# Order-only ties on VectorE in the first part of a down projection, and one weight asked for on ScalarE's queue

## The chip, the cores and the metric

The kernel runs on one core of one Trainium2 chip. The metric is the device time of one execution in microseconds (us). Before the change three runs gave 2641.38, 2643.9 and 2647.65 us; the median is 2643.9.

## The reference

Two layers of a hybrid encoder trunk: attention of four head groups, then an MLP, on 1024 tokens of 1024 features, all in float32. Cut to what matters here:

```python
for l in range(DEPTH):                                   # DEPTH = 2
    h = rms_norm(x, norm1_g[l])
    proj = h @ w_in[l]                                   # the columns of four head groups
    ...                                                  # four kinds of attention, joined as mix
    x = x + mix @ w_out[l]
    h = rms_norm(x, norm2_g[l])
    x = x + jnp.square(jax.nn.relu(h @ w_up[l])) @ w_down[l]      # 1024 -> 4096 -> 1024
return rms_norm(x, final_norm_g)
```

The change touches the product with `w_down` and one place of the product with `w_in`.

## The kernel before

**Products.** A float32 product is made of three passes of TensorE over rounded numbers (L221, L222, L223): high part of the weights by high part of the operand, high part of the weights by low part of the operand, low part of the weights by high part of the operand. A weight comes by DMA into a tile `raw` (or `ws` in the waves). ScalarE rounds it to its high part `wh` (L195), and GpSimd subtracts that from the original, which gives the low part `wl` (L189, `POOL wl<-raw,wh`). An operand (`act`, a block of the intermediate activations that was stored in DRAM) is rounded by ScalarE to `far`, and VectorE subtracts it from the original for the low part (`DVE far<-act,far`). All `tensor_tensor` operations go through one helper and carry L189.

**Down.** `mlp_down` (L1456) works in four parts j = 0 to 3. Each part is a product of two by two blocks with seven multiplications in place of eight (after Strassen and Winograd). For each of four tiles m it has the blocks a11, a12, a21 and a22 of the weights, and the differences and sums of these, which VectorE makes in place: s1 = a21 + a22 (into a `raw` tile of its own), a21' = a11 - a21, a11' = s1 - a11, a12' = a12 - a11'. The operands 1 to 7 are ready-made combinations of activation blocks. The products follow each other on TensorE in this order: a11 with operand 1 (into banks u[0] to u[3] of PSUM), a12 with operand 2 (banks p), a11' with operand 6 (u again, added to what stands there), a21' with 7 (u), a22 with 4 (u), s1 with 5 (p), a12' with 3 (p). Each product of one tile m is 12 matmuls. After each, VectorE adds the bank to the residual `x`: `x0<-u` is the addition of bank u[0] to x[0]. After the a11 products these four are called the first additions here. A bank u[m] goes on with the next product only when VectorE has read it.

**What sets the order.** TensorE's instructions stand in the order of the code. Those of the other engines are put in order by a scheduler that goes by priorities and by when their inputs should be ready; `issue_after(x)` adds for the code below it only an order on an engine (no semaphore): its instructions on the engine of `x` come behind `x`. Part j = 0 begins while the up projection before it ends: its finishing steps (`finish_up`) share VectorE and ScalarE with it. `self.settled` is the last sum of up, `self.rectified` is the rectification of its last block (`ev<-u,rb`, L1258), and in the old code the weight sums of j = 0 and the a12 additions stand behind `rectified`. `op(o)` (L1478) loads operand o through SP's queue and splits it.

**Waves.** `several` (L231) computes several groups of columns of the input projection in two halves of the inner dimension (c = 0, 1): for each half it asks for a weight of each group through SP's queue (`weights`, L202), with two `ws` buffers, so a third weight waits until GpSimd has read the first. SP's queue also carries the stores and loads by which queries and keys are rearranged through DRAM (`qb`, `kb`, `vb`, `stack`); SP issues them strictly in turn.

Of the kernel before, what the change touches and what calls it, by code (L numbers as in the profile page):

```python
# [144 lines left out]
class Trunk:  # L145
# [53 lines left out]
            nc.vector.scalar_tensor_tensor(  # L199
                out=lo, in0=src, scalar=scale, in1=hi.bitcast(F), op0=ALU.mult, op1=ALU.subtract)  # L200

    def weights(self, src, pool=None, tag="w", bufs=3, keep=None):  # L202

        pool = pool or self.wp
        n = src.shape[1]
        st = self.wp.tile([P, 4, P], F, tag="ws", bufs=2, name="ws")[:, :n]
        self.load(st, src)
        wide = n if tag != "w" else 4
        wh, wl = keep if keep is not None else (
            pool.tile([P, wide, P], R, tag=tag + p, bufs=bufs, name=tag + p)[:, :n] for p in "hl")  # L210
        self.split(wh, wl, st, eng=self.nc.gpsimd)
        return [(wh[:, k], wl[:, k]) for k in range(n)]
# [18 lines left out]
    def several(self, srcs, xs, banks, ahead=None):  # L231

        for c in range(2):
            if c:
                self.catch_up()
            ws = ahead if ahead and c == 0 else [self.weights(s[c]) for s in srcs]
            for k in range(4):
                for w, b in zip(ws, banks):
                    for n in range(2):
                        self.passes(b[n], w[k], xs[4 * c + k], slice(n * 512, n * 512 + 512),  # L240
                                    c == 0 and k == 0, c == 1 and k == 3)
# [981 lines left out]
    def mlp_up(self, l, acts):  # L1223
# [7 lines left out]
        with self.banks(q=4, u=2, p=2):  # L1231
# [90 lines left out]
            def group(q):  # L1322
                s = SimpleNamespace(q=q, c=weights(q))
                return s
# [131 lines left out]
    def mlp_down(self, l, acts):  # L1456
        nc, tc, d = self.nc, self.tc, self.d
# [3 lines left out]
        with self.banks(u=4, p=4):  # L1461
            def add(m, n, ps):
                o = self.x[m][:, N[n]]
                return self.tt(o, ps, o, ALU.add)

            for j in range(4):
                def w(m, h, tag):

                    return self.raw_weights(tag, d["w_down"][l, m, j + 4 * h])

                def raw_op(o):
                    out = []
                    for k in range(4):
                        out.append(self.piece("raw", name="act"))
                        self.load(out[k], acts[4 * j + k, o])
                    return out

                def op(o):  # L1478
                    return [self.rows_split(self.far(), t) for t in raw_op(o)]

                M = range(4)
# [3 lines left out]
                with ExitStack() as behind:  # L1485
                    if j == 0:
                        behind.enter_context(tc.issue_after(self.settled.ins))
                    b = [self.rows_split(self.far(), v) for v in t]
                    for m in M:
                        self.block(u[m], a11[m], b)  # L1490
                        added = add(m, 0, u[m])
                    rounded = self.rounded
                    a12, b = [w(m, 1, "b") for m in M], op(2)
# [4 lines left out]
                for m in M:  # L1498
                    a21.append(w(m + 4, 0, "c"))
                    a22.append(w(m + 4, 1, "c"))  # L1500
                with ExitStack() as behind:
                    if j == 0:
                        behind.enter_context(tc.issue_after(self.rectified.ins))
                    for m in M:
                        ps = self.bank("p")
                        self.block(ps, a12[m], b)
                        add(m, 0, ps)
                        s1.append(self.raw_weights("b"))
                        self.tt(s1[m], a21[m], a22[m], ALU.add)
                        sub(a21[m], a11[m], a21[m])  # L1510
                        sub(a11[m], s1[m], a11[m])
                if j == 1:
                    with tc.issue_after(added.ins):
                        self.finish_up[1]()
                b = op(6)
                for m in M:
                    self.block(u[m], a11[m], b, start=False)
                    add(m, 1, u[m])
                b = op(7)
                for m in M:  # L1520
                    self.block(u[m], a21[m], b, start=False)
                    add(m + 4, 1, u[m])
                    sub(a12[m], a12[m], a11[m])
                b = op(4)
                for m in M:
                    self.block(u[m], a22[m], b, start=False)
                    add(m + 4, 0, u[m])
                b = op(5)
# [4 lines left out]
                b = op(3)  # L1533
# [33 lines left out]
                ws = [self.weight_parts(a12[m]) for m in (2, 3)]  # L1567
# [96 lines left out]
```

## Time and profile before

| | before |
|---|---|
| median of three runs | 2643.9 us |
| the profiled execution | 2649.87 us |
| its span | 2648.1 us |
| mean granted clock of TensorE | 0.975 |
| VectorE busy | 1950.6 us |
| ScalarE busy | 1443.9 us |
| GpSimd busy | 1134.4 us |

The profile is of one execution. Rows of the timeline have the start in us, the length, the engine (PE is TensorE, DVE VectorE, ACT ScalarE, POOL GpSimd, SPq the queue of SyncE), the line, the operation, output and inputs by tile names, and in brackets the idle time just before it with what ended it. `x3` at the end of a row means three operations in a run. The span is the time from the first to the last instruction; the execution's own time is 1.8 us longer. Idle time of an engine counts only where the end depends on it.

### The profile page before, as it was taken

How to read it: one execution, taken by the hardware profiler on the slowest of the kernel's cores; microseconds unless marked ns; L12 is line 12 of the kernel's file. 1: busy time of each engine (PE TensorE's matmuls, PEld its weight loads, DVE VectorE, ACT ScalarE, POOL GpSimd, SP SyncE). 2: the span in 40 equal slices, each digit the busy share in tenths (PEclk: the TensorE clock that was granted, in tenths of full speed). 3: DMA queues.
4: the chain of work that ended last, by engine and by line, in shares of the span. 5: the costliest groups of instructions: out<-in, count | busy, mean ns of one | idle time of the engine just before them, and what ended most of it. 6: DMA issues, size and time to landing. Idle time of an engine off the chain costs nothing.

```text
span 2648.1 us, 37521 instructions
## 1 busy us (share of the span) xinstructions
PE 2524.9 (95%) x12320; PEld 2097.0 (79%) x12320; DVE 1950.6 (74%) x3403; ACT 1443.9 (55%) x2612; POOL 1134.4 (43%) x800
## 2 busy tenths in 40 slices
PE   8899998999999998999998999889999999989998
PEld 7678887877788887888877788777877888878886
DVE  6687767784986668887558777778749866678776
ACT  4577766673644444444426777666735444444445
POOL 2565642301055555555415657332011555555544
PEclk9889999999999999999998999899999999999999
DMA  5634598321144456544244445963221544665431
GB/s 169 183 88 130 146 268 260 101 90 50 63 167 153 153 192 225 154 150 140 99 119 145 118 133 155 281 206 90 80 72 35 193 147 155 234 194 165 131 116 64
DMA packets 191539, 385.00 MB, mean 145 GB/s; under 512 B 23712, under 2 KB 34928, under 8 KB 191344
## 3 DMA queue, kind: packets, MB, share of 16 engines
q1 hardware_dynamic: 176976, 356.90, 43.9%
q10 hardware_dynamic: 14368, 25.70, 2.8%
q8 instruction: 98, 1.61, 0.2%
q14 instruction: 97, 0.79, 0.1%
HBM read 261.20 MB, written 121.32 MB: 144 GB/s over the span
## 4 chain that ended last, share of the span: by engine, by line
PE 74%; DVE 10%; DMA 6%; ACT 4%; issue 3%; POOL 2%; SPq 1%; DVEq 0%; POOLq 0%; ACTq 0%
PE u L221 9%; PE u L223 9%; PE u L222 8%; PE p L223 5%; PE p L221 5%; PE p L222 5%; PE mm L221 5%; PE mm L222 5%; PE mm L223 5%; PE sb L853 3%; PE tr L889 2%; DVE p L855 2%; DVE part L189 2%; DMA bias<-in_bias 2%; ACT p L858 1%
## 5 line engine op out<-in xcount | busy, mean ns | idle before, releaser
L189 POOL TENSOR_TENSOR wl<-raw,wh 128x512 fp32r<-128x512 f32 x424 | 611.9, 1444 | 688.9 <-ACT wh L195 671.4
L195 ACT ACTIVATE wh<-raw 128x512 fp32r<-128x512 f32 x448 | 282.2, 630 | 559.0 <-PE u L222 302.0
L189 POOL TENSOR_TENSOR wl<-ws,wh 128x512 fp32r<-128x512 f32 (+1 forms) x120 | 151.9, 1267 | 420.9 <-ACT wh L195 411.4
L223 PE MATMUL u<-far,wl 128*128 128x512 f32 x768 | 300.7, 392 | 12.7 <-POOL wl L189 12.7
L221 PE MATMUL u<-far,wh 128*128 128x512 f32 x768 | 300.2, 391 | 2.3 <-ACT ev L1292 2.3
L222 PE MATMUL u<-far,wh 128*128 128x512 f32 x768 | 300.2, 391 | 0.0
L189 DVE TENSOR_TENSOR raw<-raw 128x512 f32<-128x512 f32 x256 | 227.0, 892 | 80.8 <-DMA raw<-in_w_up 45.1
L189 DVE TENSOR_TENSOR ptl<-tr,pth 128x512 fp32r<-128x512 f32 (+2 forms) x384 | 238.8, 629 | 61.2 <-ACT pth L195 59.6
L858 ACT ACTIVATE p<-p,nm 128x1024 f32<-128x1024 f32 x192 | 220.4, 1148 | 78.2 <-DVE nm L855 76.1
L195 ACT ACTIVATE pth<-tr 128x512 fp32r<-128x512 f32 (+2 forms) x384 | 206.9, 548 | 100.5 <-PE tr L889 68.4
L223 PE MATMUL p<-far,wl 128*128 128x512 f32 (+1 forms) x648 | 251.2, 388 | 3.0 <-DVE wl L189 3.0
L221 PE MATMUL p<-far,wh 128*128 128x512 f32 (+1 forms) x648 | 251.2, 388 | 0.0
L222 PE MATMUL p<-far,wh 128*128 128x512 f32 (+1 forms) x648 | 250.8, 387 | 0.0
L853 PE MATMUL sb<-stack 96*128 96x512 f32 x640 | 220.0, 426 | 15.7 <-DVE nm L855 15.1
L189 DVE TENSOR_TENSOR far<-act,far 128x512 fp32r<-128x512 f32 x224 | 202.2, 933 | 14.9 <-ACT far L195 14.9
L189 POOL TENSOR_TENSOR p<-p 128x1024 f32<-128x1024 f32 x64 | 154.6, 2416 | 104.1 <-ACT p L941 97.7
L223 PEld LDWEIGHTS u<-far,wl 128*128 128x128 f32 x768 | 145.1, 189 | 43.7 <-POOL wl L189 13.6
L221 PEld LDWEIGHTS u<-far,wh 128*128 128x128 f32 x768 | 145.0, 189 | 33.2 <-ACT ev L1292 3.1
L222 PEld LDWEIGHTS u<-far,wh 128*128 128x128 f32 x768 | 144.9, 189 | 30.8 <-DVE far L189 0.8
L889 PE MATMUL tr<-ident,p 128*128 128x128 f32 x1024 | 162.1, 279 | 7.5 <-DVE ptl L189 6.2
L221 PE MATMUL mm<-xh,wh 128*128 128x512 f32 x416 | 165.9, 399 | 2.1 <-DVE part L189 1.9
L855 DVE CUSTOM_DVE_ANT_0 p<-sb,zero 128x512 f32<-128x512 f32 x192 | 129.2, 685 | 52.3 <-PE sb L853 17.3
(256 smaller groups left out, 6148.4 us busy)
## 6 DMA issues: line engine op xcount, KB each, us to landing
act<-acts SPq DMA_DIRECT2D x224, 256.0 KB, 2.8
raw<-in_w_up SPq DMA_DIRECT2D x128, 256.0 KB, 2.7
acts<-ev SPq DMA_DIRECT2D x128, 256.0 KB, 2.2
raw<-in_w_down SPq DMA_DIRECT2D x128, 256.0 KB, 2.7
acts<-ev ACTq DMA_DIRECT2D x96, 256.0 KB, 2.5
ws<-in_w_in SPq DMA_DIRECT2D x76, 256.0 KB, 2.7
rz<-drows SPq DMA_DIRECT2D x40, 256.0 KB, 3.6
stack<-kd SPq DMA_DIRECT2D x32, 256.0 KB, 5.6
```

Source lines behind the costliest of these rows:

```text
L189: return (eng or self.nc.vector).tensor_tensor(out=out, in0=a, in1=b, op=op)
L195: self.rounded = nc.scalar.activation(hi, src, AF.Copy)
L221: mm(ps, w[0], x[0][:, sl], start=start, stop=False)
L222: mm(ps, w[0], x[1][:, sl], start=False, stop=False)
L223: mm(ps, w[1], x[0][:, sl], start=False, stop=stop)
L853: self.nc.tensor.matmul(ps, q[:, qt * P:(qt + 1) * P], k[:, sl], start=i == 0, stop=i == len(passes) - 1)
L855: self.nc.vector.tensor_tensor_reduce(out=p[:, sl], in0=ps, in1=self.zero[:, 0:1].bitcast(F).broadcast_to([P, 512]), scale=-scale, scalar= ...
L858: self.nc.scalar.activation(p, p, AF.Exp, bias=nm[:, 1:2], scale=-1.0, accum_out=z)
L889: nc.tensor.transpose(t[:, k * 256 + i * P:k * 256 + (i + 1) * P], p[:, (j * 2 + k) * P:(j * 2 + k + 1) * P], self.ident)
```

## The change

Two edits. The first is in `mlp_down` for j = 0. The operand split of `op(6)` is written ahead of the a12 products and tied behind `added`, the last of the four first additions. The work on a12 and the weight sums stays behind `rectified` for m = 0 and 1, and goes behind `added` for m = 2 and 3. The splits of operands 7 and 4 are tied behind `passed`, the last addition of the a12 products. For j = 1 to 3 `behind` does nothing.

The second is in `several`: of three weights of the second half (c = 1) the third is asked for through ScalarE's DMA queue and not through SP's.

```diff
-    def weights(self, src, pool=None, tag="w", bufs=3, keep=None):
+    def weights(self, src, pool=None, tag="w", bufs=3, keep=None, queue=None):
...
-        self.load(st, src)
+        (queue or self.nc.sync).dma_start(st, src)
...
-            ws = ahead if ahead and c == 0 else [self.weights(s[c]) for s in srcs]
+            ws = ahead if ahead and c == 0 else [self.weights(s[c], queue=self.nc.scalar if c and s is srcs[2] else None)
+                                                              for s in srcs]
...
-                with ExitStack() as behind:
-                    if j == 0:
-                        behind.enter_context(tc.issue_after(self.rectified.ins))
-                    for m in M:
+                behind = lambda ins: tc.issue_after(ins.ins) if j == 0 else ExitStack()
+                c = b
+                with behind(added):
+                    b = op(6)
+                for m in M:
+                    with behind(self.rectified if m < 2 else added):
                         ps = self.bank("p")
-                        self.block(ps, a12[m], b)
-                        add(m, 0, ps)
+                        self.block(ps, a12[m], c)
+                        passed = add(m, 0, ps)
                         s1.append(self.raw_weights("b"))
...
-                b = op(6)
                 for m in M:
                     self.block(u[m], a11[m], b, start=False)
                     add(m, 1, u[m])
-                b = op(7)
+                with behind(passed):
+                    b = op(7)
                 for m in M:
...
-                b = op(4)
+                with behind(passed):
+                    b = op(4)
```

On VectorE, in j = 0 of the first layer, the rows from the first weight sum on stood like this before (`raw<-raw,raw` are sums and differences of weights, `far<-act,far` the low parts of operand 6; `raw_10252` and `raw_10256` are a21[0] and a21[1], and `ev_10031<-p_10049` belongs to the up projection):

```order
L189 TENSOR_TENSOR raw_10286<-raw_10252,raw_10254 128x512
L189 TENSOR_TENSOR raw_10308<-raw_10256,raw_10258 128x512
L189 TENSOR_TENSOR raw_10330<-raw_10260,raw_10262 128x512
L189 TENSOR_TENSOR raw_10352<-raw_10264,raw_10266 128x512
L189 TENSOR_TENSOR ev_10031<-p_10049,ev_10031 128x512
L189 TENSOR_TENSOR raw_10252<-raw_10125,raw_10252 128x512
L189 TENSOR_TENSOR far_10364<-act_10356,far_10364 128x512
L189 TENSOR_TENSOR raw_10256<-raw_10127,raw_10256 128x512
L189 TENSOR_TENSOR far_10367<-act_10358,far_10367 128x512
L189 TENSOR_TENSOR raw_10260<-raw_10129,raw_10260 128x512
L189 TENSOR_TENSOR far_10370<-act_10360,far_10370 128x512
L189 TENSOR_TENSOR raw_10264<-raw_10131,raw_10264 128x512
```

The addition `x0<-u` came eight rows further down. After the change the rows from the same place on VectorE are these, with two sums in place of four:

```order
L189 TENSOR_TENSOR raw_10306<-raw_10252,raw_10254 128x512
L189 TENSOR_TENSOR raw_10328<-raw_10256,raw_10258 128x512
L189 TENSOR_TENSOR ev_10031<-p_10049,ev_10031 128x512
L189 TENSOR_TENSOR raw_10252<-raw_10125,raw_10252 128x512
L189 TENSOR_TENSOR raw_10256<-raw_10127,raw_10256 128x512
L189 TENSOR_TENSOR raw_10125<-raw_10306,raw_10125 128x512
L189 TENSOR_TENSOR raw_10127<-raw_10328,raw_10127 128x512
L189 TENSOR_TENSOR x0_7169<-u_10121,x0_7169 128x512
L189 TENSOR_TENSOR x1_7176<-u_10122,x1_7176 128x512
L189 TENSOR_TENSOR raw_10221<-raw_10221,raw_10125 128x512
L189 TENSOR_TENSOR x2_7183<-u_10123,x2_7183 128x512
```

The twentieth row from the rectification was `x0<-u`; now it is the eighth, and the last two sums and all low parts of operand 6 stand behind the first additions.

The second place on VectorE is the first addition after the product with operand 6, the second `x0<-u`. Before, these rows ended there (`far_10632` to `far_10641` are the low parts of operand 5):

```order
L189 TENSOR_TENSOR x1_7176<-p_10290,x1_7176 128x512
L189 TENSOR_TENSOR x2_7183<-p_10312,x2_7183 128x512
L189 TENSOR_TENSOR far_10632<-act_10624,far_10632 128x512
L189 TENSOR_TENSOR far_10635<-act_10626,far_10635 128x512
L189 TENSOR_TENSOR x3_7190<-p_10334,x3_7190 128x512
L189 TENSOR_TENSOR far_10638<-act_10628,far_10638 128x512
L189 TENSOR_TENSOR far_10641<-act_10630,far_10641 128x512
L189 TENSOR_TENSOR x0_7169<-u_10121,x0_7169 128x512
```

After the change VectorE's rows at this place are these (`far_10452` to `far_10461` are the low parts of operand 7, `far_10544` to `far_10553` those of operand 4):

```order
L189 TENSOR_TENSOR x3_7190<-p_10354,x3_7190 128x512
L189 TENSOR_TENSOR far_10452<-act_10444,far_10452 128x512
L189 TENSOR_TENSOR far_10455<-act_10446,far_10455 128x512
L189 TENSOR_TENSOR far_10458<-act_10448,far_10458 128x512
L189 TENSOR_TENSOR far_10461<-act_10450,far_10461 128x512
L189 TENSOR_TENSOR far_10544<-act_10536,far_10544 128x512
L189 TENSOR_TENSOR far_10547<-act_10538,far_10547 128x512
L189 TENSOR_TENSOR far_10550<-act_10540,far_10550 128x512
L189 TENSOR_TENSOR far_10553<-act_10542,far_10553 128x512
L189 TENSOR_TENSOR far_10638<-act_10628,far_10638 128x512
L189 TENSOR_TENSOR x0_7169<-u_10121,x0_7169 128x512
```

The eight low parts of operands 7 and 4 moved from the stretch of the first additions to the place between `x3<-p` and the second `x0<-u`. The second layer has the same order at both places.

On SP's queue, in the first layer, the third weight of the second wave stood among the rearranging transfers:

```order
L160 DMA stack_760<-kb_139 32x1024 x3
L160 DMA ws_604<-in_w_in 128x512
L160 DMA stack_767<-qb_138 32x1024
L160 DMA stack_768<-kb_139 32x1024
L160 DMA stack_767<-qb_138 32x1024
```

Now it stands on ScalarE's queue, between the roundings of the two weights before it and its own:

```order
L195 ACTIVATE wh_594<-ws_592 128x512
L195 ACTIVATE wh_600<-ws_598 128x512
L207 DMA ws_604<-in_w_in 128x512
L684 ACTIVATE both_579<-mm_574 128x8x64
L684 ACTIVATE both_588<-mm_583 128x8x64
L195 ACTIVATE wh_606<-ws_604 128x512
```

SP's rows behind it moved up by one. The lines of after.py are one higher than those of before from `several` on.

## The prediction

> **What bounds the kernel now.** I read the page first: the busy shares, the shares of the chain that ended last, and the costliest groups.
>
> ```profile
> PE 2524.9 (95%) x12320; PEld 2097.0 (79%) x12320; DVE 1950.6 (74%) x3403; ACT 1443.9 (55%) x2612; POOL 1134.4 (43%) x800
> PE 74%; DVE 10%; DMA 6%; ACT 4%; issue 3%; POOL 2%; SPq 1%; DVEq 0%; POOLq 0%; ACTq 0%
> L189 POOL TENSOR_TENSOR wl<-raw,wh 128x512 fp32r<-128x512 f32 x424 | 611.9, 1444 | 688.9 <-ACT wh L195 671.4
> L223 PE MATMUL u<-far,wl 128*128 128x512 f32 x768 | 300.7, 392 | 12.7 <-POOL wl L189 12.7
> L221 PE MATMUL tr<-xh,wh 128*128 128x512 f32 x64 | 26.0, 409 | 7.3 <-ACT wh L195 7.3
> ```
>
> TensorE is the bound, so an edit pays only where TensorE stands still. Two groups hold the stops that this change aims at: 12.7 us before the third pass of down's u products, and 7.3 us before a projection of a wave. Everything else in TensorE's rows is untouched by the diff. The timeline of TensorE and the chain of waits show the first kind.
>
> ```profile
> 1006.74 4.65 issue
> 1011.44 7.82 POOL wl L189
> 1019.30 0.80 PE u L223
> 2324.59 8.28 POOL wl L189
> 2332.91 0.80 PE L223 MATMUL u<-far,wl 128*128 128x512 f32 x1 [6.66 <-POOL wl L189]
> ```
>
> One stop per layer: 12.7 less 6.66 leaves 6.05 us in layer 0, so TensorE stood from 1013.25 to 1019.30, for the low part of a11[3], one GpSimd subtraction. GpSimd held that one subtraction open for 7.82 us. What VectorE and GpSimd did at the time:
>
> ```profile
> 1005.50 0.68 DVE L1258 SCALAR_TENSOR_TENSOR ev<-u,rb 128x512 f32<-128x512 f32 x1
> ...
> 1009.02 0.68 DVE L189 TENSOR_TENSOR ev<-p,ev 128x512 f32<-128x512 f32 x1
> 1009.62 0.68 DVE L189 TENSOR_TENSOR raw<-raw 128x512 f32<-128x512 f32 x1
> ...
> 1018.04 0.69 DVE L189 TENSOR_TENSOR x<-u,x 128x512 f32<-128x512 f32 x1
> ...
> 1024.90 1.77 DVE L189 TENSOR_TENSOR far<-act,far 128x512 fp32r<-128x512 f32 x1
> ...
> 1038.45 0.68 DVE L189 TENSOR_TENSOR x<-u,x 128x512 f32<-128x512 f32 x1
> 1040.97 0.69 DVE L189 TENSOR_TENSOR x<-u,x 128x512 f32<-128x512 f32 x1 [1.84 <-PE u L223]
> ```
>
> ```profile
> 1011.43 11.20 POOL L189 TENSOR_TENSOR wl<-raw,wh 128x512 fp32r<-128x512 f32 x3 [4.69 <-ACT wh L195]
> 1024.32 1.81 POOL L189 TENSOR_TENSOR wl<-raw,wh 128x512 fp32r<-128x512 f32 x1 [1.69 <-ACT wh L195]
> 1030.62 1.29 POOL L189 TENSOR_TENSOR wl<-raw,wh 128x512 fp32r<-128x512 f32 x1 [0.99 <-ACT wh L195]
> ```
>
> From 1009.62 to 1018.04 VectorE runs fourteen operations with two SBUF inputs without a break, one each 0.60 us (0.68 with its overlap), and GpSimd, whose subtraction also reads SBUF, gets through only when VectorE comes to x<-u at 1018.04, which reads one PSUM bank. Elsewhere the two take turns: GpSimd's 1.29 becomes 1.81, and VectorE's next operation 1.77 instead of 0.68, so a turn costs VectorE 1.09.
>
> The stop also costs clock. The view by windows (its last columns are granted clock, DMA share, GB/s):
>
> ```profile
> 1020.00:1024.00 4.00, 4.00 (x11) 3.13 (x10) 4.00 (x5) 2.30 (x4) 2.63 (x2) 0.50 0.16 61
> 1024.00:1028.00 4.00, 4.00 (x16) 3.24 (x16) 4.00 (x6) 1.39 (x3) 1.90 (x2) 0.85 0.29 84
> 2333.00:2337.00 4.00, 4.00 (x12) 3.19 (x13) 4.00 (x5) 2.05 (x4) 2.79 (x2) 0.63 0.15 52
> ```
>
> Layer 0 loses 0.35 (half of 1019.30 to 1020), 2.00 and 0.60, about 3.0 us, which makes 9.1 in all; layer 1 loses 0.37 times 4.00, 1.5, and 8.2 in all.
>
> **The change in down, by steps.** Before x3<-u (the last first-product addition) the row order of VectorE now holds no low part. Seven rows (two sums, the addition to ev, four differences) stand between the rectification at 1005.50 and x0<-u; at 0.60 each, with one turn of 0.5, x0<-u comes at about 1010.8, and its product is done by then (below). There GpSimd gets in, about when a11[3]'s high part is rounded (1010.74 before, with one far rounding fewer ahead now). Its low part is then ready at about 1012.2, against 1013.25 when TensorE asks. **The old stop goes: 9.1 and 8.2 us, 17.3 together.**
>
> What is late next? The moved work has not shrunk. VectorE's order holds 41 rows between the rectification and op6's first x0<-u in the old order, 40 in the new. The new order must also keep to TensorE's products, whose pace I take from these two of 36 rows in a line:
>
> ```profile
> 1004.48 0.39 PE L221 MATMUL u<-far,wh 128*128 128x512 f32 x1
> ...
> 1012.41 0.39 PE L223 MATMUL u<-far,wl 128*128 128x512 f32 x1
> ```
>
> 35 steps in 7.93 us are 0.2266 each, so a product of 12 matmuls takes 2.72 and four take 10.9. Without the stop the a11 products run from 1004.48 to 1015.4, the a12 products to 1026.2, op6's to 1037.1; there op7's first product wants bank u[0], which x0<-u of op6 must have read.
>
> VectorE: x3<-u cannot begin before 1015.4 and the result's flight; I take 1016.3, since a12'[0] just ahead of it waits for GpSimd's turn on a12[0]. Behind it 27 rows stand ahead of op6's x0<-u (op6's four low parts, two sums, four a21/a11 differences, two a12', four additions, op5's three, op7's four and op4's four): 28 steps of 0.60 are 16.8, to 1033.1. GpSimd needs one turn for each 2.72 us of products, nine from 1016.3 to 1041; at the mean of 0.5 and 1.09, weighted to the longer (most of what VectorE does there has two SBUF inputs), 0.9 each, they add 8.1: 1041.2. With its 0.68, **TensorE waits until 1041.9, 4.8 us, at the first op7 product, in each layer** (VectorE's rows of layer 1 are layer 0's plus 1013.01).
>
> Bounds: VectorE no later than before, 1038.45 less one row, gives a wait of 1.4; twelve turns at 1.12 and 1.74 of idle time for a12[0]'s low part, counted with 40 rows from 1005.50, give 1045, a wait of 8.7. A stop of 4.8 lies between 3.40, after which (below) the half clock cost 1.7, and 6.05, after which it cost 3.0; I take 2.4. So the new stop costs 7.2, and down gains 9.1 - 7.2 = 1.9 and 8.2 - 7.2 = 1.0: **2.9 us of 17.3**. By the bounds it is 14.5 gained (two waits of 1.4, no clock lost) to 6.1 lost (two of 8.7 with 3.0 of clock).
>
> The Trainium skill, SBUF — State Buffer, section "Who interferes with whom", says that a VectorE instruction with two SBUF inputs and a GpSimd instruction that reads SBUF exclude each other, the first to start holding the port pair for one whole instruction. The trace agrees at 1024.32 (1.81 and 1.77) but not at 1011.44: one instruction is 0.68, the wait there 6.5. By the rule alone the order of VectorE's rows would only decide who pays; it speaks against a gain here, as the 4.8 does.
>
> Other edits here cost nothing by this trace. The later low parts release operand buffers later, so SP's loads of op5's and op3's operands come later; op5's products begin at 1037.1 + 21.8 + the wait, about 1063, and its last low part is done beside 1042. If that cover went, a load (2.9 us from issue at 68.55 to 71.49, rows below) would show whole. For j of 1 and up VectorE's order is the old one.
>
> **The wave weight.** These rows are the second wave's stop in both layers, with GpSimd, SP and ScalarE ahead of it, and then what stands at the next wave:
>
> ```profile
> 60.29 2.87 POOL L189 TENSOR_TENSOR wl<-ws,wh 128x512 fp32r<-128x512 f32 x2 [9.12 <-ACT wh L195]
> 68.55 0.42 SPq L160 DMA_DIRECT2D ws<-in_w_in  x1
> 71.49 0.63 ACT L195 ACTIVATE wh<-ws 128x512 fp32r<-128x512 f32 x1 [6.67 <-DMA ws<-in_w_in]
> 72.18 0.50 PE L221 MATMUL tr<-xh,wh 128*128 128x512 f32 x1 [3.40 <-ACT wh L195]
> 1381.42 0.80 PE L221 MATMUL tr<-xh,wh 128*128 128x512 f32 x1 [3.85 <-ACT wh L195]
> 92.06 0.63 ACT L195 ACTIVATE wh<-ws 128x512 fp32r<-128x512 f32 x1 [4.36 <-DMA ws<-in_w_in]
> 1400.17 0.64 ACT L195 ACTIVATE wh<-ws 128x512 fp32r<-128x512 f32 x1 [2.24 <-DMA ws<-in_w_in]
> 95.35 1.39 DVE L189 TENSOR_TENSOR part<-p,tabs 64x512 f32<-64x512 f32 x2 [2.15 <-POOL part L189]
> 100.37 0.79 PE L853 MATMUL sb<-stack 96*128 96x512 f32 x1 [2.35 <-DVE nm L855]
> 1409.00 0.49 PE L853 MATMUL sb<-stack 96*128 96x512 f32 x1 [1.12 <-DVE nm L855]
> 1412.75 0.80 PE L853 MATMUL sb<-stack 96*128 96x512 f32 x1 [3.26 <-DVE nm L855]
> ```
>
> ```profile
> 73.00:77.00 4.00, 4.00 (x12) 3.14 (x11) 0.00 (x0) 0.00 (x0) 0.48 (x1) 0.58 1.04 345
> 81.00:85.00 4.00, 4.00 (x19) 3.33 (x18) 2.94 (x3) 3.60 (x8) 1.29 (x1) 1.00 1.04 235
> 1382.00:1387.00 5.00, 5.00 (x13) 3.92 (x12) 0.00 (x0) 0.00 (x0) 0.72 (x1) 0.50 1.03 340
> ```
>
> The third weight stands in SP's queue behind transfers that wait for others. On ScalarE's queue it is asked for about 61.7, when the first of GpSimd's two subtractions from 60.29 has read the old contents of its buffer, and lands long before TensorE wants it: the stops of 3.40 and 3.85 go, with the half clock behind them (1.7 and 2.5). But what follows is bound by transfers: the DMA engines are full from 73 to 93, ScalarE waits for the next wave's weight at 92.06 and 1400.17; GpSimd's subtraction for it stands ahead of the one for which VectorE waits 2.15 at 95.35, and VectorE is what TensorE waits for at 100.37, 1409.00 and 1412.75. These weights still go through SP. One transfer of 256 KB (0.7 us at 345 GB/s) leaves the full stretch. **I take 0.7 us a layer, 1.4 in all**; the bounds are 0 and 3.40 + 1.7 + 3.85 + 2.5 = 11.5. In the first wave TensorE didn't wait for this load: 0. ScalarE itself gives 0.42 an issue, in an idle stretch of 6.67. The scheduler also reorders much of layer 1's attention; the trace can't price that. Its stops at the next wave are 1.12 and 3.26, so I bound it by 4.4 either way and take 0.
>
> **Sum.** 2.9 + 1.4 = 4.3 us off the profiled execution's 2649.87, so 2645.6; off the median of 2643.9, which lies 6 below the profiled one, **2639.6**. A measurement of this kernel tells about 0.2%, 5.3 us, from no change (threshold 2638.6); 4.3 is just inside.
>
> **Rivals.**
> - *Both stops of down go outright.* GpSimd takes fewer or cheaper turns, VectorE reaches op6's addition by 1037. For it: the old order got there at 1038.45, and VectorE's idle time begins at 1040.97. Against: the nine turns. 17.3 + 1.4: about 2625.
> - *All is hidden.* The turns only move the stop (the rule of the page above, with the stretch's work the same): a wait of 6.05 to 6.7 at op7, and the wave's 7.3 us come back at the next wave. About 2643.
> - *Slower.* VectorE comes to op6's x0<-u later than 1042.7, from where the new stop is longer than the old. Twelve full turns and the idle 1.74 put it at 1045: a wait of 8.7 and 3.0 of clock, 11.7 twice against 17.3, 6.1 lost; with nothing from the wave 2650. For it: the new order leaves nine low parts in a row just ahead of the addition, and turns against those cost the full 1.09. Against: some of the turns fall on additions out of PSUM, which cost nothing.
>
> **How the numbers follow.** Forecast (a moved stop of some 4.8) 0.45, own range 2633 to 2645; both stops gone 0.20; hidden 0.20; slower 0.15. Faster by over 0.2%: 0.20 and somewhat under half of the 0.45, 0.40; the same: 0.45; slower: 0.15. The range reaches from 2626, which leaves out half of the first rival, to 2649, which leaves out half of the last.
>
> **What would show it.** GpSimd's low part of a11[3] should take under 2 us, with TensorE's L223 row there at no wait; a wait of some 4.8 us <-DVE x L189 should stand at L221 or L222 of u, about 24 us later, in both layers. In the wave the 3.40 and 3.85 should be gone and the stops behind it (2.35 at 100.37, 3.26 at 1412.75) longer by nearly as much. The forecast is wrong if no wait stands before op7's products, if the first stop stays, or if the stops at the next wave don't grow.
>
> The Trainium skill, TensorE: Matmul & The Clock Gate, Part 1, has the clock halve after an idle window of about 3.4 us and come back after as long a busy one; the half clock behind the stops of 3.40 and 6.05 agrees. By it a new wait under 3.4 us might cost no clock at all, and down would gain up to 2.4 more in each layer.

## The result, and the profile after

The changed kernel takes 2627.61 us in the median of six runs (2625.17 to 2633.62), the kernel before 2644.83 in the runs beside it. The ratio is 0.9938, with a 95% interval of 0.9920 to 0.9957: 0.62% faster, some 16 us. That lies inside the wide range of 2626 to 2649, but outside the forecast's own range of 2633 to 2645, and the gain is about four times the 4.3 us that were forecast.

The profiled execution of the changed kernel is the fastest of its six, that of before among the slowest of its own, so the spans (2648.1 and 2623.4) differ by 24.7. Some 7 of that arise in layer 0's attention behind the waves, where the engines have the same order in both kernels; in e_round5_op4 below, with that same order, the difference there is 2.3, so most of the 7 belongs to the two executions and not to the change. Below, a stretch is the time between the same two matmuls of TensorE, which keeps such differences out.

The page of the changed kernel, the rows that answer to those shown of before:

```profile
PE 2515.4 (96%) x12320; PEld 2088.6 (80%) x12320; DVE 1942.9 (74%) x3403; ACT 1439.0 (55%) x2612; POOL 1126.0 (43%) x800
PE 75%; DVE 9%; DMA 5%; ACT 4%; issue 3%; POOL 2%; SPq 1%; DVEq 0%; POOLq 0%; ACTq 0%
L223 PE MATMUL u<-far,wl 128*128 128x512 f32 x768 | 299.6, 390 | 5.9 <-POOL wl L189 5.9
```

The 12.7 us before down's third passes became 5.9, so not all of the stop in down went. TensorE's group rows of the changed kernel for the waves:

```profile
L221 PE MATMUL tr<-xh,wh 128*128 128x512 f32 x64 | 25.2, 396 | 0.2 <-ACT wh L195 0.2
L854 PE MATMUL sb<-stack 96*128 96x512 f32 x640 | 223.3, 430 | 23.8 <-DVE nm L856 23.3
```

and the second of them in the kernel before, where it is L853:

```profile
L853 PE MATMUL sb<-stack 96*128 96x512 f32 x640 | 220.0, 426 | 15.7 <-DVE nm L855 15.1
```

The 7.3 us of the waves went to 0.2, and 8.1 came back at the next group, at `sb<-stack`, for the most part as a stop before its first matmul, where there was none of note before (5.30 us in layer 0, 3.17 in layer 1, rows further down). Where GpSimd was kept waiting before, the timelines of the changed kernel now have these rows of VectorE, GpSimd, ScalarE, SP and TensorE (layer 0; the rectification is at 999.23, 6.27 earlier than before):

```profile
1004.53 1.28 DVE L189 TENSOR_TENSOR x<-u,x 128x512 f32<-128x512 f32 x2
...
1009.55 0.68 DVE L189 TENSOR_TENSOR x<-u,x 128x512 f32<-128x512 f32 x1
...
1023.22 1.28 DVE L189 TENSOR_TENSOR far<-act,far 128x512 fp32r<-128x512 f32 x2
1024.42 0.68 DVE L189 TENSOR_TENSOR x<-p,x 128x512 f32<-128x512 f32 x1
1025.02 5.49 DVE L189 TENSOR_TENSOR far<-act,far 128x512 fp32r<-128x512 f32 x9
1030.44 0.68 DVE L189 TENSOR_TENSOR x<-u,x 128x512 f32<-128x512 f32 x1
```

```profile
1004.30 4.61 POOL L189 TENSOR_TENSOR wl<-raw,wh 128x512 fp32r<-128x512 f32 x3 [3.84 <-ACT wh L195]
1009.81 1.30 POOL L189 TENSOR_TENSOR wl<-raw,wh 128x512 fp32r<-128x512 f32 x1 [0.91 <-ACT wh L195]
1012.53 1.48 POOL L189 TENSOR_TENSOR wl<-raw,wh 128x512 fp32r<-128x512 f32 x1 [1.42 <-ACT wh L195]
1016.40 3.43 POOL L189 TENSOR_TENSOR wl<-raw,wh 128x512 fp32r<-128x512 f32 x2 [2.40 <-ACT wh L195]
1021.21 1.54 POOL L189 TENSOR_TENSOR wl<-raw,wh 128x512 fp32r<-128x512 f32 x1 [1.37 <-ACT wh L195]
1027.75 7.38 POOL L189 TENSOR_TENSOR wl<-raw,wh 128x512 fp32r<-128x512 f32 x3 [5.00 <-ACT wh L195]
```

```profile
1018.15 2.05 SPq L160 DMA_DIRECT2D raw<-in_w_down  x2
1023.92 0.93 SPq L160 DMA_DIRECT2D act<-acts  x2
1026.52 0.63 ACT L195 ACTIVATE far<-act 128x512 fp32r<-128x512 f32 x1 [5.39 <-DMA act<-acts]
1027.06 0.62 ACT L195 ACTIVATE wh<-raw 128x512 fp32r<-128x512 f32 x1
1031.69 0.50 PE L223 MATMUL u<-far,wl 128*128 128x512 f32 x1 [2.97 <-POOL wl L189]
```

GpSimd now makes three low parts in 4.61 us from 1004.30, since x<-u stands at 1004.53, and the old stop is gone. The next one stands 96 matmuls on, at the low part of a11'[3]: 2.97 us in layer 0 and 2.94 in layer 1. Read backwards: that low part began at 1027.75 and was not done before 1031.6, because VectorE was in a run of nine low parts from 1025.02 to 1030.44. It was asked for so late because ScalarE stood 5.39 us for a load of operand 5, whose rounding is ahead of a11'[3]'s in its order. SP issued that load at 1023.92, as VectorE's low part from 1023.22 ended.

### The profile page after: what moved, and what is told of

Read it like the earlier page. It is cut to its first block, busy times and chain, and to the rows that moved or that the text cites. A ratio compares the mean times of both kernels' runs of the same rounds, so it can differ in the third digit from the quotient of the medians.

```text
span 2623.4 us, 37481 instructions
## 1 busy us (share of the span) xinstructions
PE 2515.4 (96%) x12320; PEld 2088.6 (80%) x12320; DVE 1942.9 (74%) x3403; ACT 1439.0 (55%) x2612; POOL 1126.0 (43%) x800
## 4 chain that ended last, share of the span: by engine, by line
PE 75%; DVE 9%; DMA 5%; ACT 4%; issue 3%; POOL 2%; SPq 1%; DVEq 0%; POOLq 0%; ACTq 0%
PE u L221 9%; PE u L223 9%; PE u L222 9%; PE mm L221 5%; PE p L223 5%; PE p L221 5%; PE p L222 5%; PE mm L222 5%; PE mm L223 5%; PE sb L854 3%; PE tr L890 2%; DVE p L856 2%; ACT p L859 2%; PE pv L879 2%; DVE ptl L189 1%
## 5 line engine op out<-in xcount | busy, mean ns | idle before, releaser
L189 DVE TENSOR_TENSOR far<-act,far 128x512 fp32r<-128x512 f32 x224 | 201.0, 932 | 12.7 <-ACT far L195 12.7
L189 POOL TENSOR_TENSOR p<-p 128x1024 f32<-128x1024 f32 x64 | 154.8, 2419 | 107.2 <-ACT p L942 99.8
L222 PE MATMUL mm<-xl,wh 128*128 128x512 f32 x416 | 165.2, 397 | 0.0
```

Of the source, the lines that this page charges most:

```text
L189: return (eng or self.nc.vector).tensor_tensor(out=out, in0=a, in1=b, op=op)
L222: mm(ps, w[0], x[1][:, sl], start=False, stop=False)
```

## The experiments

Stretches in us from TensorE's rows of one execution of each kernel: down in layer 0 from matmul 4750 to 5200, down in layer 1 from 10880 to 11300, and layer 1's attention from 6400 to 8700. The ratio is to the kernel before in runs on the same chip.

| kernel | ratio (95%) | down, layer 0 | down, layer 1 | attention, layer 1 |
|---|---|---|---|---|
| before | 1 | 112.6 | 105.0 | 467.5 |
| changed | 0.9938 (0.9920 to 0.9957) | 108.3 | 99.8 | 457.6 |
| e_down | 0.9954 (0.9939 to 0.9969) | 108.2 | 101.6 | 462.7 |
| e_wave | 0.9986 (0.9975 to 0.9997) | 112.6 | 105.5 | 460.1 |
| e_op6_only | 0.9962 (0.9949 to 0.9974) | 109.6 | 102.7 | 460.1 |
| e_op74_only | 0.9981 (0.9969 to 0.9993) | 110.1 | 104.0 | 464.0 |
| e_memset | 0.9985 (0.9975 to 0.9995) | 112.5 | 101.8 | 464.3 |
| e_round5 | 0.9941 (0.9925 to 0.9957) | 108.5 | 101.6 | 463.0 |
| e_round5_op4 | 0.9939 (0.9925 to 0.9953) | 104.2 | 97.9 | 457.9 |
| e_layer1_ties | 0.9980 (0.9970 to 0.9989) | 112.0 | 101.2 | 463.3 |
| e_r5op4_nowave | 0.9923 (0.9909 to 0.9936) | 105.2 | 98.0 | 456.7 |
| e_r5op4_l1wave | 0.9921 (0.9905 to 0.9938) | 107.1 | 98.6 | 456.3 |
| e_next | 0.9896 (0.9882 to 0.9910) | 104.4 | 98.5 | 455.5 |

**Which edit gains: e_down and e_wave.** The first takes the wave's edit out of the changed kernel:

```diff
-            ws = ahead if ahead and c == 0 else [self.weights(s[c], queue=self.nc.scalar if c and s is srcs[2] else None)
-                                                              for s in srcs]
+            ws = ahead if ahead and c == 0 else [self.weights(s[c]) for s in srcs]
```

> Only the edit in down, all wave weights on SP's queue. Theory A (down gives what its two places show in the profile of the changed kernel, 4.2 + 5.2 us): some 9 us below the kernel before, about 2635, and the stops of 3.4 and 3.9 us in the second waves are back. Theory C (the gain lies in the wave weight and in the new order of layer 1's attention that comes with it): 0 to 3 us below. Theory D (all of the 17 us is down's): about 2628.

The second puts those lines alone into the kernel before.

> Only the third wave weight on ScalarE's queue, down as before. Theory A: the rest of the 17 us, about 8 below the kernel before, 2637, mostly in layer 1, since in layer 0 the stop at the next wave grows by as much as the old one was. Theory C: some 14 to 17 us below. Theory D: within 2 us of the kernel before, 2643 to 2645. Both stops in down (6 and 6.7 us) stand in all three.

Down alone gave 0.46% (12.2 us of 2645), the weight alone 0.14% (3.7, with an interval of 0.8 to 6.6). C falls by e_down, and D too, since its 17 us lie above e_down's interval (8.2 to 16.1); A named 9 and 8 and had the shares wrong. The stretches of down in e_down are 4.4 and 3.4 us shorter than before, 7.8 of the 12.2. Layer 1's attention has another order than before in e_down, and the old one in e_wave, so the reordering belongs to the edit in down (to the tie of operand 6: e_op6_only has the new order, e_op74_only the old). In e_wave TensorE's rows are:

```profile
L221 PE MATMUL tr<-xh,wh 128*128 128x512 f32 x64 | 25.1, 395 | 0.0
L854 PE MATMUL sb<-stack 96*128 96x512 f32 x640 | 220.2, 426 | 22.4 <-DVE nm L856 21.6
```

7.3 us went and 6.7 came back: in TensorE's stops the weight's gain is nearly all hidden behind the next group, as forecast, though the time fell by 3.7.

**Which tie gains: e_op6_only and e_op74_only.** The first leaves the ties of operands 7 and 4 out, the second keeps those alone (both with the wave weights on SP's queue):

```diff
-                with behind(passed):
-                    b = op(7)
+                b = op(7)
...
-                with behind(passed):
-                    b = op(4)
+                b = op(4)
```

> Edit in down without the ties of operands 7 and 4 (wave weights on SP's queue). VectorE's first x0<-u is then the 11th row from the rectification, against the 8th with all ties and the 20th before. Theory A (GpSimd gets through when VectorE comes to an operation out of PSUM): the low part of a11[3] is done some 2 us later than with all ties, the first stop is 0 to 1.5 us, and since only two low parts stand ahead of op6's x0<-u in a row, no wait for a low part of a11' there: gain 8 to 13 us, at least that of down alone. Theory B (VectorE has too much to do ahead of op6's first addition): a wait of 3 to 6 us at the first op7 product in each layer, gain 3 us or less.

> Only the ties of operands 7 and 4; operand 6 and the sums as before. The first x0<-u is then the 17th row from the rectification, three rows of 0.6 us sooner than before. Theory A: the first stop shrinks by 1.8 us, to 4.3 and 4.9 us, and the late low part of a11'[3] may add a stop of up to 3; against the kernel before a gain of 0 to 4 us. Theory B: the first stop as before or shorter by 1.8, and no more waits behind it, since TensorE is late itself.

e_op6_only lost the first stop (x0<-u came 11th, as counted) and gained 0.38%, 10 us, as theory A said. But a late low part, which A had ruled out there, stood at a11'[2], in both layers (3.26 and 3.25). TensorE's timeline of e_op6_only:

```profile
1031.63 0.50 PE L221 MATMUL u<-far,wh 128*128 128x512 f32 x1 [0.47 <-ACT wh L195]
1035.62 0.80 PE L223 MATMUL u<-far,wl 128*128 128x512 f32 x1 [3.26 <-POOL wl L189]
```

e_op74_only is the more telling one. Its layer 1 has the first stop, at 4.25 us (4.9 were expected there); its layer 0, with the same order of operations up to that place, has none, but stops of 1.38 and 3.13 at a11'[3], the late low part that A had allowed for. VectorE, GpSimd and TensorE in layer 0 and then in layer 1 of e_op74_only:

```profile
1004.20 0.68 DVE L189 TENSOR_TENSOR raw<-raw 128x512 f32<-128x512 f32 x1
1004.80 1.78 DVE L189 TENSOR_TENSOR far<-act,far 128x512 fp32r<-128x512 f32 x1
...
1004.54 6.59 POOL L189 TENSOR_TENSOR wl<-raw,wh 128x512 fp32r<-128x512 f32 x4 [4.42 <-ACT wh L195]
1033.18 0.51 PE L223 MATMUL u<-far,wl 128*128 128x512 f32 x1 [3.13 <-POOL wl L189]
...
2311.04 0.69 DVE L189 TENSOR_TENSOR raw<-raw 128x512 f32<-128x512 f32 x1
2311.64 0.68 DVE L189 TENSOR_TENSOR far<-act,far 128x512 fp32r<-128x512 f32 x1
...
2316.46 0.69 DVE L189 TENSOR_TENSOR x<-u,x 128x512 f32<-128x512 f32 x1
...
2311.44 9.15 POOL L189 TENSOR_TENSOR wl<-raw,wh 128x512 fp32r<-128x512 f32 x3 [4.48 <-ACT wh L195]
```

In layer 0 GpSimd asks 0.34 us into VectorE's operation and gets in at the next one, which grows to 1.78; in layer 1 it asks 0.40 into the same operation and stands until x<-u at 2316.46. So the same order can stop TensorE or not; a shift of less than 0.1 us is the only difference that the rows show ahead of it.

**What lets GpSimd in: e_memset.** The kernel before with one operation that reads no SBUF, behind operand 6's third low part:

```diff
+                        if len(b) == 3:
+                            with tc.issue_after(self.low.ins):
+                                nc.vector.memset(self.cp.tile([P, 128], F, tag="open", name="open"), 0.0)
```

> The kernel before with one memset of 128 x 128 on VectorE (a scratch tile that nobody reads) behind operand 6's third low part, in the middle of the run in which GpSimd waited 7.8 us. Theory A (GpSimd waits until VectorE comes to an operation that reads no second SBUF input, whatever it is): GpSimd gets in at the memset, some 2 us after it asked, and a11[3]'s low part is done at most 1.5 us after TensorE wants it: stop of 0 to 1.5 us in place of 6.05 and 6.66, kernel 6 to 12 us faster than before in down, less what the new waits behind it take (up to 4 a layer). Theory E (what counts is the bank of PSUM, or a pause of VectorE): the stop stays within 0.3 us.

VectorE, GpSimd and TensorE in e_memset:

```profile
1010.99 0.68 DVE L189 TENSOR_TENSOR raw<-raw 128x512 f32<-128x512 f32 x1
1011.65 0.17 DVE L1523 MEMSET open<- 128x128 f32 x1
1011.74 3.31 DVE L189 TENSOR_TENSOR far<-act,far 128x512 fp32r<-128x512 f32 x2
1009.23 8.66 POOL L189 TENSOR_TENSOR wl<-raw,wh 128x512 fp32r<-128x512 f32 x4 [4.73 <-ACT wh L195]
1012.85 0.50 PE L223 MATMUL u<-far,wl 128*128 128x512 f32 x1 [1.82 <-POOL wl L189]
1040.96 0.77 PE L221 MATMUL u<-far,wh 128*128 128x512 f32 x1 [3.75 <-DVE x L189]
```

0.17 us of memset cut the stop from 6.05 to 1.82 (and 6.66 to 1.83 in layer 1), somewhat above the 1.5 that A allowed. Theory E falls: no bank of PSUM is needed. And here stands **the wait that the prediction forecast**: 3.75 us <-DVE x at the first op7 product. In layer 0 it gave the whole gain back (112.5 against 112.6), in layer 1, where it is 1.25, 3.2 us stayed.

**The stop that is left: e_round5 and e_round5_op4.** In the changed kernel, operand 5's roundings are tied behind that of a11'[3] (for j = 0), and in the second kernel operand 4's low parts behind op6's last addition too:

```diff
                 for m in M:
                     self.block(u[m], a11[m], b, start=False)
-                    add(m, 1, u[m])
+                    seventh = add(m, 1, u[m])
+                split_six = self.rounded
...
-                with behind(passed):
+                with behind(seventh):
                     b = op(4)
...
-                b = op(5)
+                with behind(split_six):
+                    b = op(5)
```

> The changed kernel, and operand 5's roundings on ScalarE tied for j = 0 behind the rounding of a11'[3]. Theory A (the stop of 3 us that is left stands because ScalarE waits 5.4 us for operand 5's loads ahead of that rounding, and GpSimd then meets VectorE's run of low parts): the stop of 2.97 and 2.93 goes, and 3 to 5 us a layer with it, so 2618 to 2622; if GpSimd's turns now come on time, VectorE loses up to 1.1 us on each. Theory B (without ScalarE's wait the turns make VectorE late at op6's first addition): a wait of 2 to 5 us <-DVE x at the first op7 product takes the place of the stop, and the time is that of the changed kernel within 4 us.

> As e_round5, and operand 4's low parts behind op6's last addition, which leaves four low parts in place of eight ahead of the first. Theory A: as e_round5 within 2 us. Theory B: VectorE reaches the addition 2.4 us sooner and more, the wait at op7's first product shrinks by that or goes, and this kernel is 2 to 6 us faster than e_round5.

In e_round5 ScalarE still stood for operand 5, now ahead of a21'[0]'s rounding, as its rows and those of VectorE and TensorE show:

```profile
1033.55 0.63 ACT L195 ACTIVATE far<-act 128x512 fp32r<-128x512 f32 x1 [5.25 <-DMA act<-acts]
1036.05 0.63 ACT L195 ACTIVATE far<-act 128x512 fp32r<-128x512 f32 x1 [1.87 <-DMA act<-acts]
1034.85 0.68 DVE L189 TENSOR_TENSOR x<-u,x 128x512 f32<-128x512 f32 x1
1036.59 1.13 ACT L195 ACTIVATE wh<-raw 128x512 fp32r<-128x512 f32 x2
1037.25 0.50 PE L221 MATMUL u<-far,wh 128*128 128x512 f32 x1 [2.32 <-ACT wh L195]
```

The stop at a11'[3] went, and another came one product on, at op7's first (2.32 and 0.63 us in place of 2.97; 2.03 and 0.83 in layer 1). Layer 0's stretch stayed at 108.5, layer 1's grew by 1.8. Both theories had missed that; the time agrees with B, by another mechanism: TensorE was ready for op7 at 1034.93, and x<-u was done at 1035.53, so VectorE by itself would have cost 0.6. With four low parts fewer in front of op6's first addition (e_round5_op4) the stops shrink to 0.54 and 0.63, and down is 4.0 and 1.9 us shorter than in the changed kernel. The whole time can't show it beside that of e_round5: 0.9939 and 0.9941.

**Layer 1 alone, and the weight again: e_layer1_ties, e_r5op4_nowave, e_r5op4_l1wave, e_next.** The edit in down for the last layer only; then e_round5_op4 without the weight's edit, and with it in layer 1 only; then e_round5_op4 with the latent projections' weights on ScalarE's queue too:

```diff
-        return self.weights(src[0]) + self.weights(src[1])
+        return self.weights(src[0], queue=queue) + self.weights(src[1], queue=queue)
...
-            ws = self.wtile(w_in(t))
+            ws = self.wtile(w_in(t), nc.scalar if t in (T_CQ, T_CKV, T_CQR) else None)
```

> The edit in down for layer 1 only, wave weights on SP's queue. Layer 0 and the order of layer 1's attention are those of the kernel before. Theory A (the gain of the whole edit in down, some 12 us, is made of the two places, 4.4 + 3.4 to 5 us by their stretches, and about 4 us of layer 1's attention, whose order the scheduler changed): 3 to 5 us below the kernel before. Rival (the order of layer 1's attention is worth nothing, the down places all of it): about 6 us below.

> Edit in down with operand 5's roundings and operand 4's low parts tied as in e_round5_op4, all wave weights on SP's queue. Theory A: the stretches of down keep 15 us below the kernel before and layer 1's attention its 4: 2625 to 2629; 5 to 7 us below the edit in down alone. If the wave weight is worth its 4 us, this is 4 above e_round5_op4.

> As e_r5op4_nowave, with the third wave weight on ScalarE's queue in layer 1 only. If the weight gains only in layer 1 (the stretch with its wave is 2.2 us shorter there with it, and not shorter in layer 0): 2 to 4 us below e_r5op4_nowave, equal to e_round5_op4 within 1.5 us or below it.

> As e_round5_op4, with the weights of the next groups (the three latent projections) on ScalarE's queue too. If the stops of 5 and 3 us at the next wave are bound by SP's queue, in which these weights stand behind the rearranging transfers, they shrink by 2 to 5 us in each layer. If they are bound by the DMA engines' throughput (share 1.0 in that stretch) or by VectorE, they stay within 1 us.

e_layer1_ties has layer 1's attention in the old order, and gained 0.20% (5.3 us, 2.9 to 7.9); its stretch of down is 3.8 shorter. That fits either side of its expectation. e_r5op4_nowave came out at 2624.47, 0.5 below what was expected; its ratio, 0.9923, isn't worse than e_round5_op4's with the weight, and the weight in layer 1 alone changed nothing that can be told (0.9921). So the 3.7 us of e_wave don't show again in this version. (Layer 0 of e_r5op4_l1wave has a stop of 1.78 at a11'[0] that the other kernels with the same edit there don't have.) e_next is the best kernel: 2618.23 us, 0.9896. The first stop of the group behind the wave was 5.30 in layer 0 and 3.17 in layer 1 of the changed kernel:

```profile
98.23 0.79 PE L854 MATMUL sb<-stack 96*128 96x512 f32 x1 [5.30 <-DVE nm L856]
1393.69 0.50 PE L854 MATMUL sb<-stack 96*128 96x512 f32 x1 [3.17 <-DVE nm L856]
```

(6.12 and 2.58 in e_round5_op4), and in e_next it is:

```profile
95.58 0.51 PE L854 MATMUL sb<-stack 96*128 96x512 f32 x1 [3.22 <-DVE nm L856]
1388.85 0.50 PE L854 MATMUL sb<-stack 96*128 96x512 f32 x1 [2.20 <-DVE nm L856]
```

2.1 us shorter than in the changed kernel in layer 0 and 1.0 in layer 1 (2.9 and 0.4 against e_round5_op4), while the two stops behind these stay (2.33 and 2.96 in both layers of e_next). But this stop varies by itself: in the kernels that have the third weight alone on ScalarE's queue, it is 4.24 to 7.07 in layer 0 and 2.41 to 4.35 in layer 1. So SP's queue held part of it in layer 0; in layer 1 the 2.20 is too near the others to tell. What binds the rest was not tried.

## Why the prediction was right or wrong

- **The old stop goes** (17.3 us): right, in both layers and by the mechanism named. e_memset shows it by itself.
- **TensorE waits 4.8 us at op7**: wrong for this kernel. The step that failed is VectorE's arrival, and in it the nine turns. From x3<-u at 1009.55 to op6's x0<-u at 1030.44 VectorE took 20.89; its 28 steps of 0.60 are 16.8, so the turns cost 4.1, not 8.1. Five turns fell there (GpSimd's rows from 1009.81, 1012.53, 1016.40 and 1021.21), at 0.8 each: the price of 0.9 was about right, the count was not. One had been served before (a12[1], in the row of three from 1004.30), and the three of the row from 1027.75 got in only when x0<-u came. Put on the old clock (6.27 later) x0<-u came at 1036.7, not 1041.2.
- **Why turns stayed away.** Two things kept these three back: GpSimd had nothing to subtract for 5.00 us, since ScalarE stood for a load; and when it had, VectorE's nine low parts in a row kept it out. The prediction knew that such runs shut GpSimd out, and yet counted the turns there as granted. Where GpSimd does get its turns, as in e_memset (there with the old order of rows), the wait appears, at the place named and at 3.75 us. The stop at a11'[3] hid hardly anything of such a wait: without it TensorE would have been ready for op7 at 1030.83, and x0<-u was done at 1031.12. That ScalarE's wait is what kept the wait at op7 away in the changed kernel is argued from the rows; e_round5, meant to show it, only moved ScalarE's wait.
- **A slip.** The prediction's 1013.01 between VectorE's rows of the two layers should be 1313.01 (1005.50 to 2318.51); no sum uses it.
- **Other edits here cost nothing**: wrong. Low parts that come later do release operand buffers later, as the step says; but the load that came late was wanted by ScalarE, whose order has operand 5's rounding ahead of a11'[3]'s. The step looked at when op5's products need the operand (1063), not at what stands behind it on ScalarE. It cost a stop of 2.97 and 2.94. e_round5 bears this out: with that rounding first, this stop is gone.
- **Down's gain**, 2.9 us in the sum: 4.3 and 5.2 by the stretches, 9.5 in all. The two errors above go opposite ways, and the first is the larger. With what was measured put in their place the sum comes out: 9.1 less 2.97 and 1.6 of clock is 4.5, and 8.2 less 2.94 is 5.3.
- **The weight**, 1.4 us: right in the main, since at the next group about as much came back as had gone. But the two stops named did not grow (2.35 became 2.04, 3.26 became 2.96; 1.12 in layer 1 became 2.34); most of it came as a new one ahead of them. Alone the weight measured 3.7, with 1.4 in the interval.
- **Layer 1's new order**, taken at 0 within 4.4 either way: probably worth 2 to 5 us by the stretches. Five kernels have the old order there (before, e_wave, e_op74_only, e_memset, e_layer1_ties): 463.8 us on average. The eight with the new one have 458.7. Among those with all weights on SP's queue the two groups don't overlap (463.3 to 467.5 against 456.7 to 462.7); with the weight in layer 1 on ScalarE's queue they do (460.1 in e_wave against 455.5 to 463.0). Some 4 us would make up e_down's 12.2 with the 7.8 of its stretches. Each stretch is of one execution, and no run took that order alone.
- **The rivals.** In down the one that happened is between the forecast and "both stops of down go outright": x0<-u came at 1036.7 on the old clock, by the 1037 that this rival names, and the wait at op7 did not come, but a smaller one elsewhere did. By its own sign (no wait before op7's products) the forecast is wrong. That the time lies near this rival's 2625 and still inside the range is in part luck: down gave 9.5 where the rival has 17.3, and the weight and probably layer 1's order gave more than either sum has for them.

## What to carry to other kernels

Moving work off an engine's crowded stretch is priced at the place where it lands: list what will stand in a row there, who is shut out by that run, and which in-order queues hold a load that it releases. A low-priority rounding that waits for a load holds up every urgent one behind it on its engine, so follow a late load to the engine that asks for it first, not to the product that needs it. And where one engine is starved by another's run, one very short operation that reads no SBUF, put into the run, is enough to test that reading.

## What the runs showed of the hardware

GpSimd is shut out only by a run that has lasted. Take, over the traces of all these kernels, GpSimd's low parts of weights that were asked for while VectorE stood in an operation with two SBUF inputs, not a stretched one, with another such behind it. More than 400 were asked for up to 3.66 us into VectorE's run (counted from its last pause or stretched operation), and none of them took over 1.84 us. Between 3.8 and 4.0 both happened: at 3.82 (e_op6_only) it stood until x<-u, at 3.95 (e_op74_only, layer 0) it got in. The seventeen asked for from 4.01 (layer 1 of the same kernel) to 7.0 us all stood until VectorE came to an operation with at most one SBUF input, and took 2.8 to 8.3 us. Once GpSimd is in, it stays in turn: a low part that follows at once, while VectorE's operation is still stretched by the one before, got in at the next operation, as from 1023.81 in e_round5. An addition out of PSUM inside the run, like the one at 1024.42, lets GpSimd in if it waits, but doesn't start the count afresh. What sets this limit wasn't tried.

The clock after stops near 3 us came out differently. The view by windows of the changed kernel behind the two stops of 2.97 and 2.94 us:

```profile
1032.00:1036.00 4.00, 4.00 (x12) 3.15 (x11) 4.00 (x6) 2.80 (x5) 3.33 (x3) 0.60 0.80 250
2331.40:2335.40 4.00, 3.93 (x17) 3.29 (x18) 4.00 (x6) 2.94 (x5) 4.00 (x4) 1.00 0.71 238
```

0.60 behind the first, 1.00 behind the second. The second is the odd one: of the eight stops of 2.9 to 3.3 us in down's first part over all these kernels, the other seven had a granted clock of 0.57 to 0.64 in the 4 us from their end. The Trainium skill (TensorE: Matmul & The Clock Gate, Part 1) gives an idle window of about 3.4 us as what halves the clock; the first of these stops is shorter than that and still cost 1.6 us.
